# The seven-product feed-forward of a two-layer encoder trunk: weight sums made by accumulating transfers from GpSimd, with the signs of the products turned so that the sums are additions

## The chip, the cores and the metric

The kernel runs on one core of one Trainium2 chip. The metric is the device time of one execution in microseconds (us); what is compared is the median of several runs. The engines are named as in the profile: PE (TensorE, matrix products), PEld (its weight loads), DVE (VectorE), ACT (ScalarE), POOL (GpSimd) and SP (SyncE, which here issues transfers).

## The reference

Two token groups of 512 and 256 rows, 768 in all, go through two layers of width 1024 with shared weights. Each layer has a mixer, a cross-attention into 256 memory tokens and a SwiGLU feed-forward part, with a root-mean-square norm ahead of each. All data is float32. The part that the change touches is the feed-forward one, with a hidden width of 2816:

```python
def swiglu(h, w_gate_up, w_down):
    gu = h @ w_gate_up
    g, u = gu[..., :D_FF], gu[..., D_FF:]
    return (jax.nn.silu(g) * u) @ w_down
...
        h = rms_norm(x, norm_ffn[l])
        x = x + swiglu(h, ffn_w_gate_up[l], ffn_w_down[l])
```

## The kernel before, in words

Activations are held transposed, features on the 128 partitions and the 768 tokens along the free axis. Every float32 operand of a product is split in two parts (`split`, lines 144 to 148): ACT writes a rounded high part (line 147) and DVE the rest (line 148), and a product is three matmuls, high by high, high by low and low by high (`prod`; all matmuls have line 183).

The feed-forward part of a layer (`ffn`, from line 813) works on 22 blocks of 128 hidden features. The first four blocks are done plainly. The other 18 are **hidden jobs** (line 1030): one job computes gate and up of one block for all 768 tokens as a two-by-two block product in the manner of Strassen and Winograd, with seven products in place of eight. The input features are the inner dimension and are cut in two halves; the two column halves of the result are the two halves of the tokens (`t0`, `t1`, 384 each); the two row halves are gate and up. The weights of a job come as two tiles of 128 by 1024, `a1` and `a2` (line 876, `bring`), 512 KB each, and each holds two blocks of 128 by 512, called here a11 and a12, a21 and a22. After the hidden jobs come **output jobs** (line 1074) of the same scheme with blocks 384 or 512 columns wide, which multiply by the down weights.

A product needs a left factor (weights or sums of weights) and a right factor (activations or sums of them, made once by `all_factors`, line 848). The sums of weights are four, s1 = a21 + a22, s2 = s1 - a11, a21 := a11 - a21 and a12 := a12 - s2, and DVE makes them (lines 885, 886, 887 and 891). The roles of the seven products are P1 (a11), P2 (a12), P6 (s2), P7 (the new a21), P5 (s1), P3 (the new a12) and P4 (a22). One product of a hidden job is 12 matmuls of 128 by 384, so a job is 84 matmuls.

`run` (line 909) lays the products of all jobs out in one row: P1, P2, then P3 of the job before, P6, P4 of the job before, P7, P5. While product i is written down, `left` prepares the left factor of product i + 6 (`AHEAD`), which is its split on ACT and DVE (`put`, line 867) and, at P1 and P2, the sums. When the left factor of P7 is prepared, `bring` issues the loads of the next job. P1, P6, P5 and P3 of a job add up in one bank of PSUM, P7 and P4 in another; after P1, P6, P5 the bank's state is copied out by ACT (lines 1035, 1042, 1048), after P3 by ACT's Silu (line 1053), and the next product into that bank waits for the copy. Between two products into the same bank there lie two or so of other banks.

The loads, and the parking of the finished activations in HBM, are issued from SP, in one row. Each pair of hidden jobs gives four right-factor tiles, which `finished` (line 944) stores by `keep` (line 942): three of 768 KB and one of 384 KB. `rawp` has four buffers for the weight tiles (two jobs), `wp` seven for split left factors, the pool `sum` two for s1 and s2. A framework's scheduler puts the instructions of each engine in their final order and sets the semaphore waits; each engine then runs its row strictly in order.

Of the kernel before, what the change touches and what calls it, by code (L numbers as in the profile page):

```python
# [10 lines left out]
F32 = mybir.dt.float32  # L11
# [3 lines left out]
ALU = mybir.AluOpType  # L15
AX = mybir.AxisListType

P = 128
# [4 lines left out]
T = SP + SS  # L23
# [42 lines left out]
def trunk_kernel(ctx, tc, x_in, m_in, mt_in, vec_in, cst_in, win, wf, wout, wpool, wq, wk, wv, wo, wgu, wd, out):  # L66
# [35 lines left out]
    def nm(s):  # L102
        cnt[0] += 1
        return f"{s}_{cnt[0]}"
# [29 lines left out]
    def two(ap):  # L134
        return ap.rearrange("p (b n) -> p b n", b=2)
# [28 lines left out]
    def fetch(src, n=1024):  # L164
        raw = rawp.tile([P, 1024], F32, tag="raw", name=nm("raw"))[:, :n]
        nc.sync.dma_start(raw, src)
        return raw
# [645 lines left out]
    def ffn(l, fp, tail, extra):  # L813
# [19 lines left out]
            split(two(s[:, :T]), two(s[:, T : 2 * T]), src)  # L833
            return s

        def first_factors(r, spare):

            s1 = duo_split(r[:, 0::2, :])
            t13 = chunk()
            sub(two(t13), r[:, 1::2, :], r[:, 0:2, :])  # L840
            s2 = duo_split(two(t13))
            t2 = fp.t2.tile([P, H], F32, tag="t2", name=nm("t2"))
            sub(t2, r[:, 3, :], t13[:, :H])
            th = next(spare)
            split(th[:, :H], th[:, H:T], t2)
            return s1, s2, th, t2

        def all_factors(r):

            s1, s2, th, t2 = first_factors(r, spare)  # L850
# [23 lines left out]
        WSUM = nc.vector.tensor_tensor  # L874

        def bring(job):
            job.a1, job.a2 = [fetch(src, 2 * job.cols) for src in job.src]

        def left(job, role):
            n = job.cols  # L880
            if role == "P1":
                a21, a22 = job.a2[:, :n], job.a2[:, n : 2 * n]
                job.s1, job.s2 = [fp.sum.tile([P, 512], F32, tag="sum", name=nm("sum"))[:, :n] for _ in range(2)]
                put(job, role, job.a1[:, :n])
                WSUM(job.s1, a21, a22, ALU.add)
                WSUM(job.s2, job.s1, job.a1[:, :n], ALU.subtract)
                WSUM(a21, job.a1[:, :n], a21, ALU.subtract)
            elif role == "P2":
                a12 = job.a1[:, n : 2 * n]
                put(job, role, a12)  # L890
                WSUM(a12, a12, job.s2, ALU.subtract)
            else:
                src = {"P6": job.s2, "P7": job.a2[:, :n], "P5": job.s1, "P3": job.a1[:, n : 2 * n], "P4": job.a2[:, n : 2 * n]}
                put(job, role, src[role])

        def product(job, role):

# [28 lines left out]
                if i >= 0:  # L926
                    product(*seq[i])

        def job(cols, src, right, on):
            return SimpleNamespace(cols=cols, src=src, right=right, on=on, w={}, bank={})  # L930


        spare = half_slots()
# [10 lines left out]
        def finished(q, pt):  # L944
            if q in slow:
                parked[q] = park.tile([P, 2 * SLOT], F32, tag=f"pk{l}_{q}", name=f"pk{l}_{q}")
                for i in range(2):
                    p = slot()
                    split(p[:, :T], p[:, T : 2 * T], pt[:, i * T : (i + 1) * T])
                    keep(parked[q][:, i * SLOT : (i + 1) * SLOT], p)  # L950
                return
            fs = all_factors(four(pt))
# [58 lines left out]
        def factors(k):  # L1011

            hy = slot(F32)
            scaled_x(hy[:, :T], k)
            scaled_x(hy[:, T : 2 * T], M + k)
            return right_of(all_factors(four(hy)))

        right = [factors(0)]
        pg = plain(1, 0)
        act(0, *p0)  # L1020
        right.append(factors(1))
        act(1, pg, plain(1, 1))
        right.append(factors(2))
        p2 = plain(2, 0), plain(2, 1)
        right.append(factors(3))
        act(2, *p2)
        for f in range(3, PLAIN):
            act(f, plain(f, 0), plain(f, 1))
# [1 line left out]
        def hidden_job(f):  # L1030
            st = SimpleNamespace()

            def on_p1(o):
                st.e = chunk()
                nc.scalar.activation(st.e[:, t0], o, AF.Copy)

            def on_p2(o):
                st.g = chunk()
                add(st.g[:, t0], o, st.e[:, t0])

            def on_p6(o):
                nc.scalar.activation(st.e[:, t1], o, AF.Copy)
# [19 lines left out]
            return job(512, [wgu[l, f, j] for j in range(2)], right, on)  # L1062


        def loads(g):
# [8 lines left out]
        def output_job(g, j, at):  # L1074
            n = len(groups[g])
            x0, x1 = x[2 * j], x[2 * j + 1]
            to = lambda d, t: lambda o: add(d[:, t], o, d[:, t])
            st = SimpleNamespace()

            def on_p5(o):  # L1080
                to(x1, t1)(st.b)
                to(x1, t1)(o)

            on = {
                "P1": [to(x0, t0)], "P2": [to(x0, t0)], "P6": [to(x1, t0)], "P7": [lambda o: setattr(st, "b", o)],
                "P5": [on_p5], "P3": [to(x0, t1)], "P4": [to(x1, t0)],
            }
            src = wd[l, at : at + P * 4 * n * P].rearrange("(p c) -> p c", p=P)
            return job(n * P, [src[:, : 2 * n * P], src[:, 2 * n * P :]], loaded[g], on)

        jobs = [hidden_job(f) for f in range(PLAIN, NF)]
        for i, t in enumerate(later):
# [213 lines left out]
```

## Time and profile before

| | |
|---|---|
| median of 3 runs | 1768.7 us (1768.17 to 1770.47) |
| the profiled execution's own time | 1767.83 us |
| its span in the profile | 1765.7 us |
| PE busy | 1745.6 us, 99% |
| DVE busy | 1405.5 us, 80% |
| ACT busy | 762.8 us, 43% |
| POOL busy | 2.5 us, 40 instructions, no transfer |
| DMA | 224.74 MB, mean 127 GB/s |

The profile page is of one execution. Its second part cuts the span into 40 slices; a group row gives line, engine, operation, output and input tiles, shapes, count, then busy time and the mean ns of one instruction, then the idle time of the engine just before it and what ended that. A view by windows gives the same by stretches of time, with the share of time in which the 16 DMA engines were busy and the GB/s that they moved. The copy behind P1 of a hidden job (line 1035) runs 18 times from 544.3 to 786.9 us and again from 1325.8 us on, and the last instruction of a job (line 1058) ends 18 of them at 809.0 us and 18 at 1590.4 us: that places the hidden jobs of the two layers.

### The profile page before, as it was taken

The page shows a single profiled execution, that of the slowest core. Times are in us where ns is not written, and L with a number is a line of the kernel's source. Part 1 is how long each engine was busy: PE and PEld are TensorE (multiplying, and loading weights), DVE is VectorE, ACT ScalarE, POOL GpSimd, SP SyncE. Part 2 cuts the span into 40 slices and gives each one's busy share as a digit, 9 for nine tenths or more (in the row PEclk, how much of TensorE's full clock was granted, in tenths as well). Part 3 has the DMA queues.
Part 4 walks back from the last instruction along what each step waited for, and adds up shares of the span by engine and source line. Part 5 has one row for each costly group of instructions (what it writes and reads, how often), then busy time and mean ns, then how long its engine had stood idle before and what let it go on. Part 6 is the DMA issues. An engine that isn't in the chain of part 4 may idle for free.

```text
span 1765.7 us, 26406 instructions
## 1 busy us (share of the span) xinstructions
PE 1745.6 (99%) x10362; PEld 1708.1 (97%) x10362; DVE 1405.5 (80%) x2327; ACT 762.8 (43%) x1287; POOL 2.5 (0%) x40
## 2 busy tenths in 40 slices
PE   9999999999999999999999999999999999999997
PEld 9999999999999999999999999999999999999996
DVE  7998976477788978788769984486888888879876
ACT  7233244253435555454336243352445555543331
POOL 0000000000000000000000000000000000000000
PEclk9999999999999999999999999999999999999998
DMA  7232221202214535456664332111215454547731
GB/s 255 84 108 61 92 77 48 60 22 63 60 48 173 197 135 197 137 181 247 250 234 131 95 96 63 46 48 48 60 36 189 151 189 143 197 171 273 267 86 72
DMA packets 60460, 224.74 MB, mean 127 GB/s; under 512 B 6704, under 2 KB 7984, under 8 KB 60336
## 3 DMA queue, kind: packets, MB, share of 16 engines
q1 hardware_dynamic: 60336, 223.06, 37.4%
q8 instruction: 81, 1.33, 0.3%
q14 instruction: 43, 0.35, 0.1%
HBM read 172.70 MB, written 50.33 MB: 126 GB/s over the span
## 4 chain that ended last, share of the span: by engine, by line
PE 93%; DVE 5%; DMA 1%; ACT 0%; issue 0%; SPq 0%; DVEq 0%; ACTq 0%
PE acc L183 92%; DVE s L151 1%; DVE c L279 1%; DVE s L148 1%; DVE x L323 1%; DVE s L1176 0%; DVE w L148 0%; DMA x<-in_x 0%; PE acc L751 0%; DVE x L816 0%; DMA raw<-in_wd 0%; DVE st L733 0%; DVE c L742 0%; DMA raw<-in_m 0%; DVE kl L148 0%
## 5 line engine op out<-in xcount | busy, mean ns | idle before, releaser
L183 PE MATMUL acc<-s,w 128*128 128x384 f32 x4800 | 835.4, 335 | 0.5 <-DVE x L816 0.4
L183 PEld LDWEIGHTS acc<-s,w 128*128 128x128 f32 x4800 | 831.8, 188 | 2.7 <-issue 0.8
L183 PE MATMUL acc<-s,wh 128*128 128x384 f32 (+2 forms) x2272 | 514.5, 342 | 5.7 <-DVE x L323 2.6
L183 PEld LDWEIGHTS acc<-s,wh 128*128 128x128 f32 x2272 | 403.3, 188 | 20.2 <-ACT Rx L268 3.0
L183 PE MATMUL acc<-s,wl 128*128 128x384 f32 (+2 forms) x1136 | 307.5, 341 | 0.0
L147 ACT ACTIVATE w<-raw 128x512 fp32r<-128x512 f32 (+1 forms) x304 | 181.5, 601 | 255.6 <-PE acc L183 236.0
L148 DVE TENSOR_TENSOR w<-raw,w 128x512 fp32r<-128x512 f32 (+1 forms) x304 | 196.0, 653 | 43.6 <-ACT w L147 39.7
L147 ACT ACTIVATE wh<-raw 128x1024 fp32r<-128x1024 f32 (+2 forms) x107 | 107.3, 1010 | 269.6 <-PE acc L183 252.2
L183 PEld LDWEIGHTS acc<-s,wl 128*128 128x128 f32 x1136 | 206.3, 188 | 5.3
L148 DVE TENSOR_TENSOR wl<-raw,wh 128x1024 fp32r<-128x1024 f32 (+2 forms) x105 | 122.4, 1173 | 77.7 <-PE acc L183 64.2
L183 PE MATMUL acc<-wh,s 128*128 128x256 f32 x704 | 129.0, 284 | 0.0
L816 DVE TENSOR_TENSOR x<-acc,x 128x384 f32<-128x384 f32 x168 | 92.6, 554 | 24.9 <-PE acc L183 24.2
L183 PEld LDWEIGHTS acc<-wh,s 128*128 128x128 f32 x704 | 110.7, 192 | 0.2
L323 DVE TENSOR_TENSOR x<-acc,x 128x768 f32<-128x768 f32 x80 | 76.2, 955 | 30.1 <-PE acc L183 30.0
L147 ACT ACTIVATE w<-sum 128x512 fp32r<-128x512 f32 (+1 forms) x120 | 71.9, 599 | 60.5 <-PE acc L183 42.5
L148 DVE TENSOR_TENSOR w<-sum,w 128x512 fp32r<-128x512 f32 (+1 forms) x120 | 78.4, 653 | 24.0 <-ACT w L147 23.5
L183 PE MATMUL acc<-wl,s 128*128 128x256 f32 x328 | 92.9, 283 | 0.0
L183 PE MATMUL acc<-s,s 128*128 128x512 f32 (+3 forms) x456 | 80.6, 335 | 0.0
L183 PEld LDWEIGHTS acc<-s,s 128*128 128x128 f32 x456 | 70.3, 190 | 9.5 <-issue 0.5
L433 DVE SCALAR_TENSOR_TENSOR c<-c,vec,c 128x392 f32<-128x392 f32 x124 | 70.3, 627 | 0.2
L816 DVE TENSOR_TENSOR pair<-acc,c 128x384 f32<-128x384 f32 x72 | 40.0, 556 | 32.7 <-ACT c L1048 21.0
L183 PEld LDWEIGHTS acc<-wl,s 128*128 128x128 f32 x328 | 63.0, 192 | 0.2
(146 smaller groups left out, 1541.1 us busy)
## 6 DMA issues: line engine op xcount, KB each, us to landing
raw<-in_wgu SPq DMA_DIRECT2D x88, 512.0 KB, 3.7
pk<-s SPq DMA_DIRECT2D x52, 768.0 KB, 4.1
s<-pk SPq DMA_DIRECT2D x52, 768.0 KB, 6.8
raw<-in_wd SPq DMA_DIRECT2D x32, 384.0 KB, 3.2
raw<-in_wk SPq DMA_DIRECT2D x16, 512.0 KB, 3.7
raw<-in_wv SPq DMA_DIRECT2D x16, 512.0 KB, 3.7
raw<-in_wq SPq DMA_DIRECT2D x16, 512.0 KB, 3.7
raw<-in_wo SPq DMA_DIRECT2D x16, 512.0 KB, 3.6
```

The costliest lines, as they stand in the source:

```text
L147: nc.scalar.activation(hi, src, AF.Copy)
L148: nc.vector.tensor_tensor(lo, src, asf(hi), ALU.subtract)
L151: nc.vector.scalar_tensor_tensor(lo, src, gain, asf(hi), ALU.mult, ALU.subtract)
L183: nc.tensor.matmul(o, a, b, start=start, stop=stop, skip_group_check=more)
L279: nc.vector.tensor_tensor(s, s, q, ALU.add)
L323: nc.vector.tensor_tensor(two(x[d]), halves(ps), two(x[d]), ALU.add)
L433: nc.vector.scalar_tensor_tensor(out_, src[:, a : a + CL], w, prev, ALU.mult, ALU.add)
L816: add = lambda o, a, b: nc.vector.tensor_tensor(o, a, b, ALU.add)
```

## The change

For the hidden jobs (`adds` is True) DVE makes no weight sums any more. `bring` now loads, besides `a1` and `a2`, two more tiles of 256 KB from SP: s1 starts as a copy of a21 and s2 as a copy of a11, from HBM. Then GpSimd issues transfers that add to what stands in their destination (`more`): a22 from HBM to s1, s1 from its tile to s2, a11 from HBM to the a21 part of `a2`; and at P2, behind the split of a12, s2 to the a12 part of `a1`. These are four transfers of 256 KB a job. To have only additions, the signs are turned: s2 = s1 + a11, a21 := a11 + a21, a12 := a12 + s2, and accordingly the right factors (`factors`, once `all_factors`) and some of the additions of products (`on_p5`, `on_p4`, `minus`) change sign. The output jobs (`adds` False) still make their sums on DVE, with the new signs. The pool `sum` has four buffers in place of two, and the small pool `t2` is gone: `factors` makes that sum in place in a quarter of its input.

```diff
-            f.sum, f.pair, f.t2 = pool("sum", 2), pool("pair", 2), pool("t2", 1)
+            f.sum, f.pair = pool("sum", 4), pool("pair", 2)
...
-        def first_factors(r, spare):
+        def factors(r):
...
             t13 = chunk()
-            sub(two(t13), r[:, 1::2, :], r[:, 0:2, :])
+            sub(two(t13), r[:, 0:2, :], r[:, 1::2, :])
             s2 = duo_split(two(t13))
-            t2 = fp.t2.tile([P, H], F32, tag="t2", name=nm("t2"))
-            sub(t2, r[:, 3, :], t13[:, :H])
+            b = r[:, 1, :]
+            sub(b, t13[:, H:], r[:, 0, :])
             th = next(spare)
-            split(th[:, :H], th[:, H:T], t2)
...
-            sub(r[:, 1, :], r[:, 2, :], t2)
+            split(th[:, :H], th[:, H:T], b)
+            add(b, r[:, 2, :], b)
             return s1, s2, th, duo_split(r[:, 1::2, :])
...
         def bring(job):
-            job.a1, job.a2 = [fetch(src, 2 * job.cols) for src in job.src]
+            n = job.cols
+            job.a1, job.a2 = [fetch(src, 2 * n) for src in job.src]
+            job.s1, job.s2 = [fp.sum.tile([P, 512], F32, tag="sum", name=nm("sum"))[:, :n] for _ in range(2)]
+            if job.adds:
+                nc.sync.dma_start(job.s1, job.src[1][:, :n])
+                nc.sync.dma_start(job.s2, job.src[0][:, :n])
+                more(job.s1, job.src[1][:, n : 2 * n])
+                more(job.s2, job.s1)
+                more(job.a2[:, :n], job.src[0][:, :n])
+
+        def more(o, a):
+            nc.gpsimd.dma_start(o, a, accum_op=ALU.add)
...
-                put(job, role, job.a1[:, :n])
-                WSUM(job.s1, a21, a22, ALU.add)
-                WSUM(job.s2, job.s1, job.a1[:, :n], ALU.subtract)
-                WSUM(a21, job.a1[:, :n], a21, ALU.subtract)
...
-                WSUM(a12, a12, job.s2, ALU.subtract)
...
+            put(job, role, src[role])
+            if role == "P2":
+                if job.adds:
+                    more(a12, job.s2)
+                else:
+                    add(a12, a12, job.s2)
+            elif role == "P1" and not job.adds:
+                a11, a21, a22 = job.a1[:, :n], job.a2[:, :n], job.a2[:, n : 2 * n]
+                add(job.s1, a21, a22)
+                add(job.s2, job.s1, a11)
+                add(a21, a11, a21)
...
-                add(st.u[:, t1], st.b, st.e[:, t0])
+                sub(st.u[:, t1], st.b, st.e[:, t0])
...
-                add(st.u[:, t0], o, st.e[:, t1])
+                sub(st.u[:, t0], o, st.e[:, t1])
```

On SP, in the middle of the first layer's hidden jobs, one pair of jobs before reads as follows: the weight tiles of two jobs (`raw`), then the four stores of one pair's right factors (`pk`).

```order
L166 DMA raw_5593<-in_wgu 128x1024
L166 DMA raw_5595<-in_wgu 128x1024
L166 DMA raw_5743<-in_wgu 128x1024
L166 DMA raw_5745<-in_wgu 128x1024
L942 DMA pk_3_5719<-s_5703 128x1536
L942 DMA pk_3_5719<-s_5708 128x1536
L942 DMA pk_3_5719<-s_5432 128x768
L942 DMA pk_3_5719<-s_5716 128x1536
```

The corresponding stretch of SP after the change, one pair of jobs later, where line 878 loads the start of an s1 and line 879 that of an s2:

```order
L166 DMA raw_5876<-in_wgu 128x1024
L878 DMA sum_6032<-in_wgu 128x512
L166 DMA raw_5878<-in_wgu 128x1024
L879 DMA sum_6033<-in_wgu 128x512
L166 DMA raw_6028<-in_wgu 128x1024
L878 DMA sum_6164<-in_wgu 128x512
L166 DMA raw_6030<-in_wgu 128x1024
L952 DMA pk_4_6004<-s_5988 128x1536
L952 DMA pk_4_6004<-s_5993 128x1536
L952 DMA pk_4_6004<-s_5997 128x768
L879 DMA sum_6165<-in_wgu 128x512
L952 DMA pk_4_6004<-s_6001 128x1536
```

Eight transfers of a pair of jobs became twelve. The starts of s1 and s2 (`sum_6032`, `sum_6033`) stand one job ahead of the weight tiles of their own job (`raw_6028`, `raw_6030`); an s1 start stands ahead of the second weight tile of the job before it, and an s2 start may stand among the stores.

On POOL, which had no transfer before, a later stretch of the same layer. The weight tiles of one job are `raw_6311` and `raw_6313` with the sums `sum_6315` and `sum_6316`, those of the next `raw_6443`, `raw_6445`, `sum_6447`, `sum_6448`, and `sum_6599`, `sum_6600` belong to the one after.

```order
L885 DMA sum_6447<-in_wgu 128x512
L885 DMA raw_6313<-in_wgu 128x512
L885 DMA raw_6311<-sum_6316 128x512
L885 DMA sum_6448<-sum_6447 128x512
L885 DMA sum_6599<-in_wgu 128x512
L885 DMA raw_6445<-in_wgu 128x512
L885 DMA sum_6600<-sum_6599 128x512
L885 DMA raw_6443<-sum_6448 128x512
```

Four accumulating transfers a job stand in one row, those of neighbouring jobs mixed: the sums s1 and s2 of a job stand ahead of, or around, the a21 and a12 additions of the job before it.

More of the change, by code (lines that the diff above doesn't have):

```diff
@@ L834, in duo_split @@
             return s
-        def first_factors(r, spare):
+        def factors(r):
             s1 = duo_split(r[:, 0::2, :])
             t13 = chunk()
-            sub(two(t13), r[:, 1::2, :], r[:, 0:2, :])
+            sub(two(t13), r[:, 0:2, :], r[:, 1::2, :])
             s2 = duo_split(two(t13))
-            t2 = fp.t2.tile([P, H], F32, tag="t2", name=nm("t2"))
-            sub(t2, r[:, 3, :], t13[:, :H])
+            b = r[:, 1, :]
+            sub(b, t13[:, H:], r[:, 0, :])
             th = next(spare)
-            split(th[:, :H], th[:, H:T], t2)
-            return s1, s2, th, t2
-        def all_factors(r):
-            s1, s2, th, t2 = first_factors(r, spare)
-            sub(r[:, 1, :], r[:, 2, :], t2)
+            split(th[:, :H], th[:, H:T], b)
+            add(b, r[:, 2, :], b)
             return s1, s2, th, duo_split(r[:, 1::2, :])
@@ L876, in bring @@
         def bring(job):
-            job.a1, job.a2 = [fetch(src, 2 * job.cols) for src in job.src]
+            n = job.cols
[9 more added lines that the diff above has]
+            nc.gpsimd.dma_start(o, a, accum_op=ALU.add)
         def left(job, role):
             n = job.cols
-            if role == "P1":
-                a21, a22 = job.a2[:, :n], job.a2[:, n : 2 * n]
-                job.s1, job.s2 = [fp.sum.tile([P, 512], F32, tag="sum", name=nm("sum"))[:, :n] for _ in range(2)]
-                put(job, role, job.a1[:, :n])
[L885 to L894, printed above, removed]
+            a12 = job.a1[:, n : 2 * n]
+            src = {
+                "P1": job.a1[:, :n], "P2": a12, "P6": job.s2, "P7": job.a2[:, :n], "P5": job.s1, "P3": a12,
+                "P4": job.a2[:, n : 2 * n],
+            }
+            put(job, role, src[role])
[9 more added lines that the diff above has]
+                add(a21, a11, a21)
         def product(job, role):
@@ L927, in run, with job @@
                     product(*seq[i])
-        def job(cols, src, right, on):
-            return SimpleNamespace(cols=cols, src=src, right=right, on=on, w={}, bank={})
+        def job(cols, src, right, on, adds):
+            return SimpleNamespace(cols=cols, src=src, right=right, on=on, w={}, bank={}, adds=adds)
         spare = half_slots()
@@ L951, in finished @@
                 return
-            fs = all_factors(four(pt))
+            fs = factors(four(pt))
             if q >= NPAIR - 2:
@@ L1009, in scaled_x, with factors_of @@
             nc.vector.scalar_tensor_tensor(o, x[kk], v("ffn", l * KD + kk), R, ALU.mult, ALU.mult)
-        def factors(k):
+        def factors_of(k):
             hy = slot(F32)
@@ L1015, in factors @@
             scaled_x(hy[:, T : 2 * T], M + k)
-            return right_of(all_factors(four(hy)))
-        right = [factors(0)]
+            return right_of(factors(four(hy)))
+        right = [factors_of(0)]
         pg = plain(1, 0)
         act(0, *p0)
-        right.append(factors(1))
+        right.append(factors_of(1))
         act(1, pg, plain(1, 1))
-        right.append(factors(2))
+        right.append(factors_of(2))
         p2 = plain(2, 0), plain(2, 1)
-        right.append(factors(3))
+        right.append(factors_of(3))
         act(2, *p2)
@@ L1061, in hidden_job @@
             on = {"P1": [on_p1], "P2": [on_p2], "P6": [on_p6], "P7": [on_p7], "P5": [on_p5], "P3": [on_p3], "P4": [on_p4]}
-            return job(512, [wgu[l, f, j] for j in range(2)], right, on)
+            return job(512, [wgu[l, f, j] for j in range(2)], right, on, True)
         def loads(g):
@@ L1076, in output_job @@
             x0, x1 = x[2 * j], x[2 * j + 1]
-            to = lambda d, t: lambda o: add(d[:, t], o, d[:, t])
+            plus = lambda d, t: lambda o: add(d[:, t], o, d[:, t])
+            minus = lambda d, t: lambda o: sub(d[:, t], d[:, t], o)
             st = SimpleNamespace()
             def on_p5(o):
-                to(x1, t1)(st.b)
-                to(x1, t1)(o)
+                plus(x1, t1)(st.b)
+                minus(x1, t1)(o)
             on = {
-                "P1": [to(x0, t0)], "P2": [to(x0, t0)], "P6": [to(x1, t0)], "P7": [lambda o: setattr(st, "b", o)],
-                "P5": [on_p5], "P3": [to(x0, t1)], "P4": [to(x1, t0)],
+                "P1": [plus(x0, t0)], "P2": [plus(x0, t0)], "P6": [minus(x1, t0)], "P7": [lambda o: setattr(st, "b", o)],
+                "P5": [on_p5], "P3": [plus(x0, t1)], "P4": [plus(x1, t0)],
             }
             src = wd[l, at : at + P * 4 * n * P].rearrange("(p c) -> p c", p=P)
-            return job(n * P, [src[:, : 2 * n * P], src[:, 2 * n * P :]], loaded[g], on)
+            return job(n * P, [src[:, : 2 * n * P], src[:, 2 * n * P :]], loaded[g], on, False)
         jobs = [hidden_job(f) for f in range(PLAIN, NF)]
```

## The prediction

> **What bounds the kernel now.** I read the page's first part, then the chain of waits in order of time, then the windows over the hidden jobs. The page names one engine that is nearly always busy:
>
> ```profile
> span 1765.7 us, 26406 instructions
> ...
> PE 1745.6 (99%) x10362; PEld 1708.1 (97%) x10362; DVE 1405.5 (80%) x2327; ACT 762.8 (43%) x1287; POOL 2.5 (0%) x40
> ```
>
> PE stands idle for 1765.7 - 1745.6 = 20.1 us of the span. Where, the chain tells: through the hidden jobs it stays on PE's matmuls and on nothing else (columns: start, length, what).
>
> ```profile
> 479.82 398.49 PE acc L183 x2296
> ...
> 1252.78 491.22 PE acc L183 x2817
> ```
>
> Both pieces contain all hidden jobs of their layer. The windows of 40 us inside the first layer's hidden jobs show the same from the engines' side; the last three columns are the granted clock, the busy share of the DMA engines and their GB/s.
>
> ```profile
> core 0: us, PE busy (x) PEld busy (x) DVE busy (x) ACT busy (x) POOL busy (x), PEclk, DMA share, GB/s
> 560.00:600.00 40.00, 40.00 (x232) 40.00 (x232) 37.16 (x62) 22.02 (x41) 0.00 (x0) 1.00 0.64 231
> 600.00:640.00 40.00, 40.00 (x233) 40.00 (x232) 32.26 (x50) 21.61 (x40) 0.00 (x0) 1.00 0.43 149
> 640.00:680.00 40.00, 40.00 (x233) 40.00 (x232) 34.53 (x56) 21.25 (x40) 0.00 (x0) 1.00 0.56 204
> 680.00:720.00 40.00, 40.00 (x233) 40.00 (x232) 31.40 (x49) 20.27 (x37) 0.00 (x0) 1.00 0.38 136
> 720.00:760.00 40.00, 40.00 (x232) 40.00 (x232) 33.08 (x52) 22.71 (x41) 0.00 (x0) 1.00 0.51 181
> 760.00:800.00 40.00, 40.00 (x233) 40.00 (x232) 31.54 (x51) 19.76 (x38) 0.00 (x0) 1.00 0.55 194
> sum 240.00, PE 240.00 PEld 240.00 DVE 199.96 ACT 127.62 POOL 0.00; mean PE 40.00 PEld 40.00 DVE 33.33 ACT 21.27 POOL 0.00
> ```
>
> PE has no gap in 240 us, at full clock, and starts 232 or 233 matmuls per window whether DVE is busy for 37.16 us or for 31.40, and whether the DMA engines are busy for 0.64 or 0.38 of it. So PE is at its own pace of 40.00 / 232.7 = 0.172 us a matmul, a job of 84 takes 14.44 us and the 36 jobs 520 us. What is taken off DVE here cannot shorten that.
>
> **The change part by part.** *DVE's sums go.* Four groups leave the hidden jobs (36 of the 44 in each row; the other eight belong to output jobs):
>
> ```profile
> L891 DVE TENSOR_TENSOR raw<-raw,sum 128x512 f32<-128x512 f32 x44 | 30.3, 690 | 0.7
> L886 DVE TENSOR_TENSOR sum<-sum,raw 128x512 f32<-128x512 f32 x44 | 30.3, 688 | 0.7
> L885 DVE TENSOR_TENSOR sum<-raw 128x512 f32<-128x512 f32 x44 | 30.2, 687 | 11.0 <-DMA raw<-in_wd 8.5 <-DMA raw<-in_wgu 2.3
> L887 DVE TENSOR_TENSOR raw<-raw,raw 128x512 f32<-128x512 f32 x44 | 30.2, 686 | 0.1
> ```
>
> That is 36 x 4 x 0.688 = 99 us of DVE time, all of it beside a PE without gaps: gain on the path 0. DVE's busy time should fall to about 1306 us.
>
> *The signs.* An addition becomes a subtraction and the other way round, as many instructions and shapes as before. Addition (L816) and subtraction (L817) of one shape cost the same:
>
> ```profile
> L816 DVE TENSOR_TENSOR c<-acc,c 128x384 f32<-128x384 f32 x36 | 19.9, 552 | 0.0
> ...
> L817 DVE TENSOR_TENSOR t<-pair,c 128x384 f32<-128x384 f32 x20 | 11.0, 552 | 0.0
> ```
>
> The in-place sum in `factors` overwrites a quarter that DVE has to finish splitting first, and DVE runs in order anyway. Both edits: 0.
>
> *Transfers.* The nearest rows for the new ones are the plain loads (the 256 KB load of `in_m` is the size of each new transfer; the last column is from issue to landing), and the issue itself on SP, of 0.33 us:
>
> ```profile
> raw<-in_wgu SPq DMA_DIRECT2D x88, 512.0 KB, 3.7
> pk<-s SPq DMA_DIRECT2D x52, 768.0 KB, 4.1
> ...
> raw<-in_m SPq DMA_DIRECT2D x16, 256.0 KB, 2.7
> ```
> ```profile
> L166 SPq DMA_DIRECT2D raw<-in_wgu x88: 327/328/431, 413.9 to 1548.6; - x88
> ```
>
> No transfer of this trace is issued from GpSimd and none adds. First the volume. In the six windows the engines are busy for (0.64 + 0.43 + 0.56 + 0.38 + 0.51 + 0.55) / 6 = 0.512 at a mean of (231 + 149 + 204 + 136 + 181 + 194) / 6 = 182.5 GB/s, so a full share is about 356 GB/s. The two plain starts of s1 and s2, 524 KB per 14.44 us or 36.3 GB/s, add 0.102. The four accumulating transfers carry 1049 KB, 72.6 GB/s, and each pass of these bytes through the engines adds 0.204. A transfer that adds must at least fetch its source, so it is no cheaper than a plain one: one pass is the lower end, share 0.82. It fetches source and destination and writes the sum; if nothing of this overlaps, it is three passes, share 1.22. I take two, because a plain transfer also reads and writes and is charged once here: share 1.02. Then the engines need 2% more time than PE: 0.021 x 14.44 x 36 = 11 us. The ends are 0 and 0.224 x 14.44 x 36 = 116 us.
>
> The Trainium skill, page "Collectives: The Full Stack", section "The bandwidth ceiling: the fold count and why AG ≠ RS ≠ AR", says that a reducing transfer makes two reads through the same read ring and so moves about half as much (it gives 32.35 against 62.28 GB/s); estimated from that page it is 1.93 passes, share 1.01, and this term would be 3 us. No run here shows it yet.
>
> Next the waits. The split of P6's left factor now waits for three transfers in a chain (start of s1, a22 onto it, s1 onto s2), that of P7's for two (a2, a11 onto it), and both stand in ACT's row ahead of the copies that free PE's banks:
>
> ```profile
> L1042 ACT ACTIVATE c<-acc x36: 472/492/493, 547.3 to 1574.2; 128x384 f32<-128x384 f32 x36
> its engine sat idle before it (us, times) until:
>   PE acc L183: 28.2, 33
> ```
>
> Now ACT waits for PE ahead of that copy, 33 times of 36, which is the harmless direction. PE needs the copy two products later, 2 x 12 x 0.172 = 4.1 us. So ACT may be held that long and no longer. The chain for P6, at 2.7 us for the start and 3.7 us (a 512 KB row, two passes) for each addition, with three issues of 0.33 us, is 11 us. The buffer of s1 is freed by P5's split two jobs earlier, 11 places in the row of products, 11 x 2.06 = 22.7 us: this chain fits. For P7, `a2`'s buffer is freed by P4's split, 8 places ahead, 16.5 us; load and addition take 3.7 + 3.7 + 0.7 = 8.1 us. But SP's row now puts an s1 start that waits for a later buffer ahead of this load, and a pair's stores among them:
>
> ```profile
> 668.63 5.13 SPq L942 DMA_DIRECT2D pk<-s  x4
> 676.92 17.83 SPq L166 DMA_DIRECT2D raw<-in_wgu  x4
> ```
>
> The four stores are 3 x 768 + 384 = 2688 KB, 2.75 MB, or 7.7 us of all engines at 356 GB/s. With them 16.5 - 8.1 - 7.7 = 0.7 us are left, and a full DMA leaves nothing. Where stores and the P7 chain meet, once a pair of jobs, ACT is held past its 4.1 us by something between 0 and about 1.2 us (half of the s1 start's 2.7 us); I take 0.6 us, 18 times: 11 us. Behind the held ACT stand the copies for P1, P6 and P5 and the later splits; PE waits for the copies first, since six left factors are ahead.
>
> At a layer's first two hidden jobs POOL has the additions of both in one row and no lead yet; each start can cost one addition's 3.7 us or nothing; I take 1.5 us, twice: 3 us. GpSimd's issue time is unknown; at SP's 0.33 us it is in the sums above. At three times that, 1 us, P7's chain would be 0.7 us longer, 18 x 0.7 = 12 us more, which I keep for the range. GpSimd has nothing else to do in these windows (POOL 0.00), so nobody else is queued behind its waits.
>
> The sum is 0 + 0 + 11 + 11 + 3 = 25 us, made against the profiled execution's own time of 1767.8 us, its span and 2.1 us around it: 1793 us. That execution lies 0.9 us under the median of the runs shown, which I leave out.
>
> **The rivals.** *All hidden (not slower).* If an addition costs the DMA engines one pass, their share is 0.82, the queue empties in every job, 7.7 us of stores are done before they hurt, and ACT is never held beyond 4.1 us. It decides at 1.9 passes, where 0.614 + 0.204 x p reaches 1. For it: the first layer ran at 0.64 for 40 us without a gap in PE. Against: two reads. Time 1768, at most 3 us more from the two starts.
>
> *Three passes.* Reads and write follow each other, and 2 KB rows leave no overlap: 1767.8 + 116 + 11 + 3 = 1898 us, DMA full in all windows of the hidden jobs.
>
> *GpSimd held back by DVE.* If GpSimd can write its commands only while DVE is off, then with DVE at 33.33 of 40 us, less 4 x 0.688 x 40 / 14.44 = 7.6, it gets 0.36 of the time, an issue of 1 us (three times SP's) becomes 2.8 us, and the addition in P7's chain comes 2.8 - 0.33 = 2.5 us later in each pair: 1793 + 18 x 2.5 = 1838 us. The skill's page "SBUF — State Buffer", section "SBUF: two separate sides", has such a lock, but infers that two-input DVE operations, which these are, leave the write side free.
>
> *A gain.* PE's 20.1 us of gaps lie outside the hidden jobs; a shifted order at their borders could give back some 4 us: 1764.
>
> **How the numbers follow.** The forecast has a chance of 0.60, all hidden 0.20, three passes 0.12, the held GpSimd 0.05, a gain 0.03. Faster by over 0.2% (3.5 us, about what a measurement of this kernel can tell from no change) is 0.03, within it 0.20, slower 0.60 + 0.12 + 0.05 = 0.77. The range begins at 1767 us, so that all hidden is in it, and ends between two and three passes: at 2.5 the volume costs 0.122 x 520 = 64 us, with 14 us 1846. Three passes and the gain are left out, 0.15.
>
> **What would show it.** Right: 144 transfers on POOL at L885; DMA share near 1 in the windows between 560 and 800 us; DVE near 1306 us; gaps in PE inside the hidden jobs of both layers whose releaser is an ACT copy, with ACT before it waiting in a split for a transfer into `raw` or `sum`; 228 or fewer matmuls per 40 us. Wrong: a share near 0.8 and PE at 232 per window (all hidden), or 190 per window (three passes). If PE has gaps at a share of 0.8, the waits alone are the cause and my first term is void.

## The result, and the profile after

| | before | after |
|---|---|---|
| median | 1768.43 us (4 runs, 1768.01 to 1770.47) | 1833.08 us (4 runs, 1831.12 to 1835.14) |
| span of the profiled execution | 1765.7 us | 1829.3 us |
| PE busy, and idle in the span | 1745.6, 20.1 us | 1768.6, 60.7 us |

The ratio is 1.0363 (95% interval 1.0345 to 1.0381): 65 us slower, where 25 were forecast. The page of the changed kernel, its first part and the row of the queue of GpSimd's transfers (packets, MB, share of 16 engines' span):

```profile
PE 1768.6 (97%) x10362; PEld 1723.4 (94%) x10362; DVE 1317.0 (72%) x2183; ACT 754.2 (41%) x1287; POOL 129.2 (7%) x184
...
q0 software_dynamic: 20736, 37.76, 11.9%
```

The 144 sums have gone from DVE (2327 - 2183) and come to POOL (184 - 40). The loss has two halves on PE: 40.6 us more of gaps, and 23.0 us more of busy time for the same 10362 matmuls; together the 63.6 us between the spans. The windows over the first layer's hidden jobs, with the columns of those of before:

```profile
560.00:600.00 40.00, 34.82 (x182) 34.18 (x181) 23.98 (x39) 18.00 (x34) 7.89 (x9) 0.91 0.99 296
600.00:640.00 40.00, 37.92 (x219) 37.60 (x217) 20.98 (x33) 15.85 (x29) 9.68 (x11) 1.00 0.88 241
640.00:680.00 40.00, 38.12 (x203) 37.80 (x204) 23.79 (x37) 20.28 (x39) 7.96 (x9) 0.91 0.85 236
680.00:720.00 40.00, 36.69 (x211) 36.11 (x210) 22.38 (x35) 16.11 (x31) 9.59 (x11) 1.00 0.88 228
720.00:760.00 40.00, 35.96 (x191) 35.28 (x190) 25.19 (x40) 19.79 (x38) 7.66 (x10) 0.91 0.86 234
760.00:800.00 40.00, 39.17 (x226) 38.75 (x225) 23.17 (x36) 17.42 (x34) 9.15 (x11) 1.00 0.91 277
```

PE starts 182 to 226 matmuls where it started 232 or 233, and no engine is full: behind the first window the DMA share is 0.85 to 0.91. The clock is 0.91 in three windows, 3 x 0.09 x 40 = 11 us of the busy half of the loss. What PE waits for stands in the table of waits (us in total, times, longest):

```profile
ACT w L147 <- DMA raw<-in_wgu: 164.9, 36, 10.5
...
PE acc L183 <- ACT c L1058: 38.1, 17, 4.0
```

ACT stands in a split for a transfer into `raw` 36 times. By the trace of each wait, 24 of them, 154.5 us, are for the addition onto a21; the other 12, none over 2.0 us, are for a plain load. PE then waits 17 times, about once a pair of jobs, for the copy behind P5 (line 1058) that stands behind the split in ACT's row. This is the chain that the prediction named. But why is the addition so late, and late even in jobs without stores? The waits of SP's row between 560 and 800 us give it away:

```profile
SPq L878 <- DMA raw<-sum: 117.0, 13, 11.8
```

For half of these 240 us SP stands at one instruction, the start of an s1, until an addition of s2 onto a12 has landed (`raw<-sum`). Three rounds of it in the timeline of SP (start, length, what, how many; `pk` are the stores):

```profile
690.32 0.33 SPq L878 DMA_DIRECT2D sum<-in_wgu  x1
690.75 0.37 SPq L166 DMA_DIRECT2D raw<-in_wgu  x1
691.22 1.76 SPq L952 DMA_DIRECT2D pk<-s  x3
...
707.98 0.33 SPq L878 DMA_DIRECT2D sum<-in_wgu  x1
708.42 0.37 SPq L166 DMA_DIRECT2D raw<-in_wgu  x1
...
723.24 0.33 SPq L878 DMA_DIRECT2D sum<-in_wgu  x1
...
724.13 2.18 SPq L952 DMA_DIRECT2D pk<-s  x3
...
741.91 0.33 SPq L878 DMA_DIRECT2D sum<-in_wgu  x1
```

and the first two of them on POOL (in brackets the idle time ahead and what ended it):

```profile
694.28 0.88 POOL L885 DMA_DIRECT2D sum<-in_wgu  x1 [7.22 <-DMA sum<-in_wgu]
696.26 0.87 POOL L885 DMA_DIRECT2D raw<-in_wgu  x1 [1.10 <-DVE w L148]
696.91 1.12 POOL L885 DMA_DIRECT2D raw<-sum  x1
704.31 0.88 POOL L885 DMA_DIRECT2D sum<-sum  x1 [6.29 <-DMA sum<-in_wgu]
711.67 0.88 POOL L885 DMA_DIRECT2D sum<-in_wgu  x1 [6.47 <-DMA sum<-in_wgu]
713.09 0.87 POOL L885 DMA_DIRECT2D raw<-in_wgu  x1 [0.55 <-DMA sum<-in_wgu]
718.32 0.88 POOL L885 DMA_DIRECT2D sum<-sum  x1 [4.36 <-issue]
718.97 1.12 POOL L885 DMA_DIRECT2D raw<-sum  x1
```

Read both together, they are a circle. The start at 690.32 must land before POOL can add to that s1 (694.28). Behind that addition stands the one onto a21 (696.26), whose load SP could issue only behind the start (690.75; in this round a split on DVE came last, by a little), and behind it the addition onto a12 (696.91). When this has landed, SP is released: 707.98, 17.7 us after 690.32. By this wait, the buffer of the next start is the s2 that the addition was reading. The second round has no stores in it, but the addition onto s2 (718.32) is now ahead of the one onto a12, and it takes 15.3 us. The third has stores again and takes 18.7 us. The mean of the first two, 16.5 us, is more than the 14.44 us that PE takes for a job. The starts of both layers, from the rows of line 878 in two stretches (least, median and longest issue in ns, then first and last start):

```profile
L878 SPq DMA_DIRECT2D sum<-in_wgu x12: 327/328/333, 602.9 to 787.8; - x12
...
L878 SPq DMA_DIRECT2D sum<-in_wgu x14: 327/328/333, 1388.5 to 1602.6; - x14
```

That is 184.9 / 11 = 16.8 us a round and 214.1 / 13 = 16.5. Beyond 14.44 it makes 26 us a layer, 52 of the 63.6; most of the rest lies where the hidden jobs begin. In the trace each of these 24 rounds ends with a start within 0.15 us of the landing of an addition onto a12. But they are not alike: behind a first one of 20.6 us, the 11 with a pair's stores in them take 17.0 to 18.8 us, 18.1 in the mean, and the 12 without 13.7 to 15.9, 14.9 in the mean. So 11 x 3.7 = 41 of the 52 us come in the rounds with stores, where the addition onto a12 takes 9.8 to 12.0 us to land, and not 3.6 to 5.8 as in the others.

The other half is the clock. Here are PE's timeline after two such gaps and a window of 10 us behind each; the first begins 3 us behind the gap's end:

```profile
706.86 29.68 PE L183 MATMUL acc<-s,w 128*128 128x384 f32 x168 [3.31 <-ACT c L1058]
740.58 19.61 PE L183 MATMUL acc<-s,w 128*128 128x384 f32 x97 [4.04 <-ACT c L1058]
```
```profile
710.00:720.00 10.00, 10.00 (x60) 10.00 (x59) 5.34 (x9) 3.89 (x8) 3.43 (x4) 1.00 0.77 195
...
740.00:750.00 10.00, 9.42 (x40) 9.43 (x41) 5.25 (x9) 5.41 (x12) 1.74 (x2) 0.70 0.75 197
```

Behind the gap of 4.04 us PE starts 40 matmuls in 10 us at a granted clock of 0.70, behind that of 3.31 us 60 at full clock.

### The profile page after: what moved, and what is told of

Same layout as the page of the kernel before. It is cut to its first block, busy times and chain, and to the rows that moved or that the text cites. A ratio compares the mean times of both kernels' runs of the same rounds, so it can differ in the third digit from the quotient of the medians.

```text
span 1829.3 us, 26854 instructions
## 1 busy us (share of the span) xinstructions
PE 1768.6 (97%) x10362; PEld 1723.4 (94%) x10362; DVE 1317.0 (72%) x2183; ACT 754.2 (41%) x1287; POOL 129.2 (7%) x184
## 3 DMA queue, kind: packets, MB, share of 16 engines
q0 software_dynamic: 20736, 37.76, 11.9%
## 4 chain that ended last, share of the span: by engine, by line
PE 67%; DMA 16%; DVE 11%; issue 3%; ACT 2%; POOL 0%; SPq 0%; ACTq 0%; POOLq 0%; DVEq 0%
PE acc L183 67%; DMA raw<-in_wgu 10%; DMA sum<-in_wgu 2%; DMA raw<-sum 2%; DVE s L148 2%; DVE w L148 2%; DMA raw<-in_wd 2%; DVE s L151 1%; DVE c L279 1%; ACT s L147 1%; DVE x L323 1%; DMA sum<-sum 1%; DVE x L816 0%; DVE sum L816 0%; DVE s L1187 0%
## 5 line engine op out<-in xcount | busy, mean ns | idle before, releaser
L183 PE MATMUL acc<-s,w 128*128 128x384 f32 x4800 | 858.6, 339 | 40.1 <-ACT c L1058 38.1
L183 PEld LDWEIGHTS acc<-s,w 128*128 128x128 f32 x4800 | 847.7, 191 | 49.7 <-ACT c L1058 44.2
L885 POOL DMA_DIRECT2D sum<-in_wgu x36 | 32.2, 895 | 783.0 <-PE acc L183 389.9
L816 DVE TENSOR_TENSOR x<-acc,x 128x384 f32<-128x384 f32 x120 | 65.9, 552 | 16.0 <-PE acc L183 15.4
```

The lines of the kernel that those rows point to most:

```text
L183: nc.tensor.matmul(o, a, b, start=start, stop=stop, skip_group_check=more)
L816: add = lambda o, a, b: nc.vector.tensor_tensor(o, a, b, ALU.add)
L885: nc.gpsimd.dma_start(o, a, accum_op=ALU.add)
```

## The experiments

Three theories stand against each other. **Ring** (or circle): the round just read, over two engines' rows and a buffer, paces the jobs. **Volume**: the DMA engines have more to move than fits beside PE, my first term. **Held ACT**: P7's load and addition by themselves are too long for their place, and ACT in its split holds PE's copies, my second term as it was reasoned. Kernels are told from the changed kernel unless a line says otherwise.

| run | what it is | median us | ratio to before |
|---|---|---|---|
| signs_only | all sums back on DVE | 1771.71 | 1.0014 [1.0005, 1.0024] |
| a12_on_dve | one of the four sums back on DVE | 1779.45 | 1.0055 [1.0034, 1.0076] |
| a21_on_dve | another | 1813.55 | 1.0246 [1.0230, 1.0262] |
| s1_on_dve | another | 1844.28 | 1.0422 [1.0406, 1.0438] |
| volume_beside | transfers that nobody waits for | 1773.34 | 1.0028 [1.0019, 1.0038] |
| copies_on_dve | PE's copies out of ACT's row | 1834.86 | 1.0372 [1.0338, 1.0406] |
| slots18 | control with 18 activation buffers | 1832.29 | 1.0352 [1.0331, 1.0373] |
| slots18_sum6 | six sum buffers | 1819.30 | 1.0297 [1.0274, 1.0319] |
| rows_pinned_sum4 | two rows' order set by hand | 1816.22 | 1.0270 [1.0254, 1.0285] |
| rows_pinned_sum6 | the same, six sum buffers | 1788.07 | 1.0108 [1.0091, 1.0125] |
| plain_transfers | copies in place of additions | 1775.35 | 1.0036 [1.0024, 1.0048] |
| pinned_late_start | three jobs a layer on DVE | 1781.71 | 1.0071 [1.0056, 1.0086] |
| late_start | three jobs a layer on DVE | 1824.91 | 1.0320 [1.0299, 1.0340] |
| idle_gaps | the kernel before with gaps made by ACT | 1800.25, one run | - |

**One sum at a time.** Each of three runs gives one sum of every hidden job back to DVE: a12 (the link that ends the round), a21 (P7's addition), or s1 (the first link).

```diff
a12_on_dve
-                if job.adds:
-                    more(a12, job.s2)
-                else:
-                    add(a12, a12, job.s2)
+                add(a12, a12, job.s2)
a21_on_dve
-                more(job.a2[:, :n], job.src[0][:, :n])
...
+                add(a21, a11, a21)
s1_on_dve
-                more(job.s1, job.src[1][:, n : 2 * n])
+                add(job.s1, job.s1, job.a2[:, n : 2 * n])
```

> The a12 sum of the hidden jobs goes back to DVE; the other three additions stay on GpSimd. Ring theory (each start of an s1 on SP waits until an a12 addition has landed; behind it on SP stands the a2 load, behind that on GpSimd the a21 addition and the next a12 addition, so the round trip sets the time of a job): the ring is cut, 1768 to 1780 us, starts of s1 no longer issued right behind a landing on the GpSimd queue. Volume theory (the DMA engines' work per job sets its time): one addition less is 8 x 178 ns = 1.4 us of 14.4 us work per job and engine, about 1781 to 1790 us, the same for each addition that is taken away. Held-ACT theory (the wait for a21 alone): unchanged, about 1830 us.

> The a21 sum of the hidden jobs goes back to DVE; the other three additions stay on GpSimd. Ring theory: the long ring through the a2 load and a21 is gone, but the a12 additions still stand behind other additions on GpSimd and the s1 starts behind a12; a shorter ring remains, 1775 to 1815 us. Volume theory: the same as without a12, 1781 to 1790 us. Held-ACT theory: P7's split no longer waits for a transfer, 1768 to 1775 us.

> s1 is still started by a load, but a22 is added to it by DVE; the other three additions stay on GpSimd. Ring theory: a12, s1 start, a2 load, a21 and a12 again are all still there, so no better than 1825 us, perhaps worse, since s2 now waits for a2 too. Volume theory: as for the other two, 1781 to 1790 us. Held-ACT theory: about 1830 us.

Without the a12 link 53.6 us of the 65 are gone, though P7's load and addition are as they were; without P7's addition only 20 are. That is against held ACT. In a21_on_dve a shorter circle is left, since SP still stands at the start of an s1 until an addition onto a12 has landed:

```profile
SPq L878 <- DMA raw<-sum: 77.5, 13, 8.0
```

Without the s1 addition it is slower still, with fewer bytes. One window of a12_on_dve and one of s1_on_dve:

```profile
640.00:680.00 40.00, 40.00 (x233) 40.00 (x232) 31.27 (x48) 22.73 (x41) 7.67 (x9) 1.00 0.94 280
```
```profile
680.00:720.00 40.00, 36.29 (x197) 35.33 (x196) 23.33 (x37) 16.57 (x32) 7.08 (x8) 0.96 0.72 202
```

PE runs at its own pace at a share of 0.94 and falls behind at 0.72. The volume is not what PE loses by.

**The bytes by themselves.** DVE makes all sums, with the new signs, and GpSimd issues six transfers a job into tiles that nobody reads, four of them adding.

```diff
+            if job.idle:
+                d1, d2 = [fp.idle.tile([P, 512], F32, tag=g, name=nm("idle")) for g in ("ia", "ib")]
+                nc.gpsimd.dma_start(d1, job.src[1][:, :n])
+                nc.gpsimd.dma_start(d2, job.src[0][:, :n])
+                more(d1, job.src[1][:, n : 2 * n])
+                more(d2, job.src[1][:, :n])
+                more(d1, job.src[0][:, :n])
+                more(d2, job.src[0][:, n : 2 * n])
```

> DVE makes all sums with the new signs, and GpSimd issues the same six transfers per hidden job (two plain starts, four additions) into two tiles that nobody reads; so the traffic is that of the change and no engine waits for it until the stage ends. Ring theory and held-ACT theory: 1768 to 1775 us, no gaps in PE in the hidden jobs. Volume theory: loads and stores are late for the same reason as in the change, 1800 to 1835 us with a DMA share near 0.9.

Two windows of it:

```profile
560.00:600.00 40.00, 39.08 (x224) 38.47 (x224) 34.39 (x57) 21.23 (x39) 9.27 (x12) 1.00 0.99 312
...
640.00:680.00 40.00, 40.00 (x233) 40.00 (x232) 35.28 (x57) 23.27 (x42) 9.83 (x13) 1.00 0.94 285
```

At 0.99 and 312 GB/s PE starts 224 matmuls, at 0.94 all 233. The bytes cost 4.9 us in all (1773.34 less the 1768.44 us of the kernel before in the same runs), and that with the signs in them. Nothing paces these transfers, so they are through before 760 us in the first layer: they load the DMA engines more densely than the change does, not less.

**The signs alone.** `job(..., on, False)` for the hidden jobs.

> The changed kernel with the four sums of the hidden jobs given back to DVE, so that only the signs, the in-place sum of the right factors and the four sum buffers are left of the change. All theories: 1767 to 1770 us, PE without gaps in the hidden jobs, DVE near 1406 us. If it comes out more than 4 us above the kernel before, part of the loss lies in the signs and the ring of waits has been charged with too much.

2.9 us over the 1768.85 us of before in the same runs: a trace of a loss, over my range of 1767 to 1770 us and under the 4 us that I had set. The profiled execution shows no place for it: PE is at 40.00 us in all six windows.

**PE's copies out of ACT's row.** The three copies behind P1, P6 and P5 are made by DVE (`tensor_copy`).

> The changed kernel with the three copies behind P1, P6 and P5 made by DVE, so that PE's banks no longer wait for an ACT that stands in a split. Held-ACT theory (only the copies in ACT's row hand the delay to PE): 1770 to 1785 us. Ring theory: a round still takes 16.5 us where PE needs 14.44, so it must be lost somewhere; PE waits for the left factors themselves in place of the copies, and the time stays at 1815 to 1840 us.

No gain, as the ring theory has it. PE's wait went over to the copy's new place:

```profile
PE acc L183 <- DVE c L1058: 32.8, 15, 6.7
```

Held ACT is how the delay reaches PE, not what makes it.

**More sum buffers.** Six sum buffers go with 18 activation buffers in place of 19, so there is a control with 18 and four.

```diff
-SLOTS = 19
+SLOTS = 18
...
-            f.sum, f.pair = pool("sum", 4), pool("pair", 2)
+            f.sum, f.pair = pool("sum", 6), pool("pair", 2)
```

> A control: the changed kernel with 18 activation buffers where it has 19, which frees the room that the next run needs. All theories: 1825 to 1840 us, like the changed kernel; if it differs by more, the next run is compared with this one and not with the changed kernel.

> The control with six sum buffers where the changed kernel has four: all four additions of each job stay with the transfers, and as many bytes move. Ring theory (the start of s1 two jobs later sits on the buffer of this job's s2 and so waits until s2 has been added onto a12): the starts now wait for a buffer that came free a job earlier, the round may take 14.4 us longer than now, and the time falls to 1770 to 1785 us with PE at 228 or more matmuls in most windows of 40 us. Volume theory: no change against the control. Held-ACT theory (P7's two transfers by themselves are too long for their place): no change against the control, 1820 us or more.

13 us gained, where I expected 50 or so. The scheduler used the two buffers to issue the starts a job earlier and set them in front of the same loads; SP stands as long as ever:

```profile
SPq L878 <- DMA raw<-sum: 124.5, 13, 12.3
```

A start that is issued a job earlier doesn't make the round shorter. By this run alone ring and volume could not be told apart; it led to the next two.

**The order of the rows.** On SP the starts of a job go behind the a2 load of the job before, on GpSimd its additions for s1 and s2 behind the a21 addition of the job before. These are orders of issue without a wait. One run has four sum buffers (and 19 activation buffers), one six (and 18).

```diff
+            load = nc.sync.dma_start(job.a2, job.src[1])
...
+                with behind("a2"):
                     nc.sync.dma_start(job.s1, job.src[1][:, :n])
                     nc.sync.dma_start(job.s2, job.src[0][:, :n])
+                with behind("a21"):
                     more(job.s1, job.src[1][:, n : 2 * n])
                     more(job.s2, job.s1)
+                last["a21"] = more(job.a2[:, :n], job.src[0][:, :n])
+            last["a2"] = load
...
+        def behind(name):
+            return tc.issue_after(last[name].ins) if name in last else nullcontext()
```

> All four additions stay with the transfers, the same bytes move, and nothing goes back to DVE; only the order of two rows is set: on SP the two starts of a job stand behind the a2 load of the job before, on GpSimd its two additions for s1 and s2 stand behind the a21 addition of the job before. Six sum buffers and 18 activation buffers, as in the run with six buffers that is 1819 us. A start now waits for an addition that is two jobs old, and nothing that the job in between needs stands behind it. Ring theory (what paces the jobs is the circle: start waits for the addition onto a12, that stands on GpSimd behind an addition that waits for a load, that stands on SP behind a start): the circle is cut, 1770 to 1790 us, PE at 228 or more matmuls in most windows of 40 us, DMA share as before at 0.8 to 1.0. Volume theory, and the theory that P7's load and addition by themselves are too long for their place: no change, 1810 to 1830 us, since both are untouched. If it lies between, at 1790 to 1810, the circle is one of two causes.

> The same two pinned rows with four sum buffers (and 19 activation buffers) as in the changed kernel. Ring theory: with four buffers a start waits for the addition onto a12 of the job just before, and this stands behind both additions for s1 and s2, so a circle of one job is left: start 3.5 to 4 us, first addition 5, second in the row, addition onto a12 5, longer with the stores, 15 us or more: 1805 to 1850 us. If it is as fast as the run with six buffers, the order of the rows alone was the cause and the buffers were not.

With four buffers a start still waits for the addition onto a12 of the job just before, and SP's longest wait is still that one:

```profile
SPq L881 <- DMA raw<-sum: 99.1, 13, 10.3
```

With six it is gone, and 45 of the 65 us with it, while every addition and every byte is where the change put it. SP's longest wait is now one at a weight load for an addition onto a12 (67.1 us between 560 and 800), and PE has no gap from it. Windows of the run with six, and its starts of s1 in part of them:

```profile
640.00:680.00 40.00, 40.00 (x233) 40.00 (x232) 24.87 (x38) 20.70 (x38) 10.36 (x12) 1.00 0.98 253
680.00:720.00 40.00, 40.00 (x233) 40.00 (x232) 26.20 (x42) 21.27 (x39) 9.00 (x11) 1.00 0.98 280
720.00:760.00 40.00, 40.00 (x232) 40.00 (x231) 25.49 (x40) 21.51 (x40) 9.68 (x11) 1.00 1.00 291
```
```profile
L881 SPq DMA_DIRECT2D sum<-in_wgu x5: 383/385/442, 649.4 to 707.7; - x5
```

The round is 58.3 / 4 = 14.6 us, PE's own, and PE has no gap at a share of 0.98 to 1.00. The stores are all there too, and here they hold nobody up. So the circle is shown as the cause of these 45 us, the volume as none.

**Plain copies.** `dma_start(o, a)` without `accum_op`: this kernel leaves out the additions.

> The changed kernel with its GpSimd transfers made plain copies: this leaves out the additions, so that the sums are not formed. Same rows, waits and issues, each transfer one pass in place of two. Ring theory: the round has an addition onto a12 and one for a21 or s1 in it, each about 1 to 2.5 us shorter, so the round comes to 13 to 14.5 us and the time to 1770 to 1795 us. If the time of GpSimd's issue were what counts (0.87 us against SP's 0.33), little would change: 1815 us or more.

The round closes inside PE's pace when its transfers are shorter: from 614.2 to 756.2 us the starts come every 14.2 us. The queue's row, the issue of one kind (min/median/max ns) and two landings between 560 and 800 us:

```profile
q0 software_dynamic: 11520, 37.76, 6.1%
```
```profile
L885 POOL DMA_DIRECT2D raw<-sum x36: 536/536/547, 526.7 to 1563.3; - x36
```
```profile
raw<-in_wgu POOLq DMA_DIRECT2D x16, 256.0 KB, 3.7
raw<-sum POOLq DMA_DIRECT2D x16, 256.0 KB, 5.1
```

In the changed kernel the same rows of that stretch are:

```profile
raw<-in_wgu POOLq DMA_DIRECT2D x15, 256.0 KB, 7.5
raw<-sum POOLq DMA_DIRECT2D x15, 256.0 KB, 5.8
```

An adding a21 transfer takes 3.8 us more here, the issue of an addition onto a12 about 0.6 us more (1.12 against 0.54). Both lie in the round; this run doesn't part them.

**The start of a layer's hidden jobs.** The first three hidden jobs of each layer keep their sums on DVE (`f >= PLAIN + 3` for `adds`), once with the rows pinned and six buffers, once in the changed kernel.

> The run with both rows pinned and six sum buffers (1788 us), with the sums of the first three hidden jobs of each layer given back to DVE; the other 15 jobs of a layer keep their four additions on transfers. In the run without this, PE's gaps inside the hidden jobs lie in the first two or three jobs of each layer alone (2.7 and 4.9 us in the first layer, 1.4 and 4.3 us in the second) with 13.7 us at half clock behind them. Start theory (the first jobs have no lead: their chains of three transfers begin only when the layer's buffers come free, and the 20 us that are left over the kernel before are theirs): 1768 to 1774 us. Rival (each hidden job still pays a little for its additions, so the loss goes with the number of jobs): 20 us x 15/18 are left, 1782 to 1788 us.

> The changed kernel itself with the sums of the first three hidden jobs of each layer given back to DVE, rows not pinned, four sum buffers. Ring theory with a separate start term: the starts' 15 to 20 us go, but the circle paces the other 15 jobs of a layer as before, and these have more lead at first: 1805 to 1822 us. If the loss all came from a bad start that is never caught up: 1768 to 1780 us. If the start has nothing to do with it: 65 x 15/18 = 54 us are left, 1822 us or more.

1781.71 us: 6.4 less than without it, just under the rival's range and well over the start theory's. But the loss is in one place. PE's timeline of this run in the first layer, where the first jobs whose sums come by transfer begin, and a later window:

```profile
569.81 19.58 PE L183 MATMUL acc<-s,w 128*128 128x384 f32 x112
597.42 102.85 PE L183 MATMUL acc<-s,w 128*128 128x384 f32 x577 [8.03 <-ACT c L1055]
```
```profile
720.00:760.00 40.00, 40.00 (x233) 40.00 (x232) 25.50 (x40) 20.58 (x38) 9.69 (x11) 1.00 1.01 293
```

So there is no price per job once the rows run with a lead, at a share of 1.01; the start cost was not removed but moved to where the transfers now begin, in the first layer. In the second layer the run has no such gap. Why one crossing costs 8 us and the other nothing stays open. The unpinned run came to 1824.91 us: it lost 8 us of the start and kept the circle, over my ring range of 1805 to 1822.

**The clock.** The kernel before, with f + 4 ACT copies of P5's result in hidden jobs of odd f.

```diff
+                if f % 2:
+                    h = fp.hold.tile([P, 512], F32, tag="hold", name=nm("hold"))
+                    for _ in range(f + 4):
+                        nc.scalar.activation(h[:, :H], o, AF.Copy)
```

> The kernel before, with extra ACT copies of P5's result in every second hidden job, 9 copies in the first and two more each time up to 25, each 0.49 us; nothing else is changed. PE can do without ACT for 4.1 us, so its gaps grow from about 0 to 8 us. Theory of the clock: after a gap longer than some length near 2.5 to 3.5 us the granted clock stands at 0.5 for 3.4 or 6.8 us, after a shorter one it stays at 1.0; so the matmuls behind a long gap take twice their time and a gap costs up to 3.4 us more than it lasts. Rival: the clock falls with load on the DMA engines or with GpSimd's additions, and not with gaps; then there is no half clock here, where no transfer adds.

The gaps came out smaller than planned: in each layer one only is over 2 us, and it lies just behind the hidden jobs. PE's timeline and windows of 10 us around it:

```profile
813.09 16.24 PE L183 MATMUL acc<-s,w 128*128 128x384 f32 x89 [1.48 <-ACT w L147]
831.99 2.61 PE L183 MATMUL acc<-s,w 128*128 128x384 f32 x7 [2.66 <-DVE w L148]
```
```profile
820.00:830.00 10.00, 9.33 (x54) 8.97 (x52) 7.73 (x14) 4.51 (x9) 0.00 (x0) 1.00 1.00 386
830.00:840.00 10.00, 7.34 (x26) 6.84 (x27) 7.22 (x16) 2.22 (x5) 0.00 (x0) 0.66 0.49 145
```

Behind the gap of 2.66 us the clock is 0.66 in the window, behind the 1.48 us it is full, and POOL issues nothing at all. So the half clock follows the gap and doesn't need the additions; nor does it follow the DMA's load, which is at 1.00 just ahead of it here, since rows_pinned_sum6 ran at 0.98 to 1.00 for 120 us with a clock of 1.00. It tells the length only roughly: 2.66 us was enough here and 2.07 us in the changed kernel (the gap ends at 592.4 us; clock 0.83 from 592 to 602), but 3.31 us there was not. These gaps account for little of this run's 32 us over the kernel before; where the rest lies was not followed. The Trainium skill, page "TensorE: Matmul & The Clock Gate", section "Part 1: The HAM clock gate (the "warmup" mystery)", has the clock fall to half after an idle stretch of about 3.4 us, by a window that runs free of the program. These runs agree in kind but not in the length, since 2.07 and 2.66 us were enough. The free window may account for the spread, which no run here shows.

No run is faster than the kernel before. Its PE has no gap in the hidden jobs, so freed DVE time buys nothing there.

## Why the prediction was right in sign and wrong in size

**Right**: the sign (slower); DVE's 99 us bring nothing; 144 transfers on POOL; the releaser, an ACT copy with ACT in a split for a transfer into `raw`; 228 or fewer matmuls in every window. DVE came to 1317 us where I said 1306. My last sentence came true in kind: behind the first window PE has gaps at a share of 0.85 to 0.91 (I had named 0.8), so the first term is void. The share near 1 that I had named as a sign came in the first window only: spread over a round of 16.5 us, my 1.02 is 1.02 x 14.44 / 16.5 = 0.89.

**The volume, 11 us forecast, 5 at most.** The price was right. From the page's rows of the software queue: adding, 0.119 x 16 x 1829.3 / 37.76 = 92 us of an engine per MB; plain, in plain_transfers, 0.061 x 16 x 1771.9 / 37.76 = 46. That is two passes. The Trainium skill, page "Collectives: The Full Stack", section "The bandwidth ceiling: the fold count and why AG ≠ RS ≠ AR", gives a measured ratio of 1.93 between a collective that copies and one that reduces, which reads two sources. The trace's 2.0 agrees with it. What was wrong is the step from a share of 1.02 to lost time: rows_pinned_sum6 runs at 0.98 to 1.00 and loses nothing there.

**The waits, 11 us forecast, 45 (by the pinned rows) to 52 (by the rounds) measured.** This is the step that failed. The prediction put it so: "SP's row now puts an s1 start that waits for a later buffer ahead of this load", and charged it half of a start's 2.7 us, once a pair. The place was right: PE waits for the copy behind P5 17 times, where I said 18. The price was not: SP stands at such a start for 117.0 / 13 = 9.0 us. I asked how long P7's chain is against its 16.5 us place, and whether s1's chain fits its 22.7 us, each by itself, and took the buffer of s1 to be freed by P5's split. In the trace the start waits until the addition onto a12 has landed, and that addition stands on POOL behind the very transfers that the start holds up. Followed once round, start, addition, a21, a12 and the next start, the rows of the order that the front of this document shows would have closed. By the landings that I used, the round is 2.7 + 3.7 + 3.7 = 10.1 us, or 2.7 + 3.7 + 7.7 = 14.1 us with the stores: just inside 14.44, with nothing to spare for an issue. Landings under load (7.5 and 5.8 us in the rows of the changed kernel above) and issues of 0.87 to 1.12 us, which I had kept for the range, bring it to 14.9 us without the stores and 18.1 us with them. So most of the price does fall once a pair, but it is some 3.7 us and not 0.6, and the round between, at 14.9 us, wins nothing back.

**The starts, 3 us forecast, up to 20 measured.** What rows_pinned_sum6 still loses lies in the first two or three jobs of a layer. Its first window, beside the later ones above:

```profile
560.00:600.00 40.00, 33.13 (x176) 32.49 (x175) 25.58 (x41) 18.53 (x36) 6.97 (x8) 0.93 0.97 301
```

I had priced one chain's wait of 1.5 us, not gaps of several and the half clock behind them.

**The clock, not in the prediction.** The prediction took PE's 0.172 us a matmul as fixed; 23 us more of PE's busy time were measured. In the changed kernel, and this is argued and not shown, it is not on top of the circle's loss, since PE would wait for the next left factor anyway.

## What to carry to other kernels

When a step moves from an engine to queues, follow the order of every queue and every buffer's release until it comes back to where it began: a circle that is longer in the mean than the bound engine's own time per job sets the pace, however idle each of its parts is. Its sign in a profile is a queue that stands in one kind of wait in every job (here 117 of 240 us) while no engine is full. The cure is the order of the rows together with the buffers: either alone gave back 13 to 17 us, both 45.

## What the runs showed of the hardware

- A gap of 2.07 to 4.04 us on PE can be followed by some us at a lower clock (0.83, 0.66 and 0.70 in windows of 10 us, behind gaps of 2.07, 2.66 and 4.04 us), so a gap costs more than it lasts; 3.31 us once cost nothing further, 1.48 us neither.
- An adding transfer from GpSimd holds a DMA engine 92 us per MB, a plain one 46; its issue takes 0.87 us, 1.12 us from tile to tile, against 0.54 us plain and 0.33 us from SP.
- The DMA engines at a share of 0.98 to 1.01 over 40 us didn't slow PE, as long as the transfers had a lead.
